# Expert weights in pieces of 4 contraction blocks by 512 columns instead of 8 by 256, and six units of work per expert instead of eight

## The chip, the cores and the metric

The kernel runs on one core of a Trainium2 chip. The metric is the device time of one execution in microseconds (us), the median of several runs. The engines are PE (TensorE, matrix products; its weight loads are shown apart as PEld), DVE (VectorE), ACT (ScalarE), POOL (GpSimd) and SP (SyncE, which here issues transfers). Each engine works through its own list of instructions in order and waits for the others by semaphores. Transfers run on 16 DMA engines.

## The reference

One layer of a diffusion trunk: a token mixer (windowed attention beside a long convolution), then a mixture of 32 experts of which each of 1024 tokens uses four. The change lies in the experts alone. Cut to them (D is 1024, D_FF is 1024, w1 is 1024 x 2048 and w2 is 1024 x 1024 per expert, all float32):

```python
logits = xt @ router_w + router_b
top_vals, top_idx = lax.top_k(logits, 4)
gate = softmax(top_vals)
...
for each expert e, on the tokens tok that chose it:
    hb = x[tok] @ w1[e] + b1[e]
    glu, lin = split(hb, 2)
    glu = minimum(glu, 7.0); lin = clip(lin, -7.0, 7.0)
    act = glu * sigmoid(1.702 * glu) * (lin + 1.0)
    acc[tok] += (act @ w2[e] + b2[e]) * weight
```

So column f of the gate half of w1 and column 1024 + f of its linear half meet in one value of `act`, and every value of `hb` is a sum over all 1024 rows of w1, which are 8 contraction blocks of 128 rows.

## The kernel before

**Stages.** Until about 1128 us the program computes the token mixer and the routing; the experts run from there to about 2503 us; the last 50 us add up and normalise. The change touches the experts.

**Experts by rank.** Experts are sorted by the number of their tokens; the expert of rank r gets `CAPS[r]` columns (line 68), from 416 down to 32. Two are in work at a time, in two lanes: lane 0 takes ranks 0, 1, 2, ... (416, 384, 304, 256, ... columns), lane 1 takes them from the end (32, 32, ... up to 128). `plan` (lines 75 to 91) lays down in which order units of the two lanes follow each other: it adds up a price for PE and one for DMA per unit and takes lane 0 when PE has less than DMA. An expert has 8 units: 4 of w1, each with a gate piece and a linear piece, then 4 of w2, each with one piece.

**Pieces.** A piece is 1 MB of float32 weights: all 8 contraction blocks by 256 columns, so that each transferred row is 1 KB (`w1`, `w2` in `wjobs`, lines 336 to 338). `jload` (line 301) has SP load it into one of 5 `raw` buffers. `jsplit` (line 307) turns it into two float16 parts, in two halves: ACT writes the high part `wh` (line 315), DVE then the low part `wl` (line 317); there are 5 buffers of each. `jget` hands out the next piece, `jahead(2)` (line 319) has the next two split behind a unit's matmuls.

**A unit of w1** (lines 366 to 402). For each 128 columns of the piece `mm3` (line 339) adds 24 matmuls in PSUM: 8 contraction blocks, each with high times high, high times low and low times high (the experts of 56 columns and fewer join two of them). Gate and linear products go to PSUM side by side. Then follows the activation: DVE adds the bias to both (`sg` line 387, `sl` line 388), ACT takes the sigmoid (`ss`, line 391), DVE multiplies (lines 392 and 393), ACT and DVE write the high and the low part of the result (`ah` line 397, `al` line 398). These are the moving operand of w2.

**A unit of w2** (lines 404 to 418) has 2 times 24 matmuls on one piece; ACT writes the result `yT`. At an expert's end `rows_out` transposes it and adds it to the tokens' rows with an indirect transfer from POOL (line 431).

**The next expert's tokens** are fetched beside the units of the one before it in the same lane, by steps (`prep_`, lines 288 to 295): step 1 builds one-hot rows `S`; at step 2 (and 3) PE multiplies them with the row table (line 262), DVE makes indices `gi` of it, and POOL starts the indirect transfer of the tokens' rows into `g` (line 277); at steps 5 to 7 (4 to 7 for more than 256 columns) PE transposes `g` (`tr`, line 286) and ACT writes it as `xT`, the moving operand of w1. Step u is emitted ahead of unit u (line 472). The biases `br` of an expert are loaded by SP (lines 355 and 356) and transposed by PE (line 358) at its start.

**Order.** The tile framework lays down each engine's order when the program is built, from the order of the calls, priorities and its own view of when operands are ready. The chip's engines then keep that order.

Of the kernel before, what the change touches and what calls it, by code (L numbers as in the profile page):

```python
# [19 lines left out]
ALU = mybir.AluOpType  # L20
# [73 lines left out]
assert sorted((r,u) for l,r,u in PLAN)==[(r,u) for r in range(NE) for u in range(8)]  # L94
class Moe:
# [205 lines left out]
    def jload(s):  # L301
        nc=s.nc
        src=s.jobs[s.jl_n]
        raw=s.ww.tile([128,8,256],F32,name="raw",bufs=s.NRAW)
        nc.sync.dma_start(raw,src())
        s.jraw[s.jl_n]=raw; s.jl_n+=1
    def jsplit(s):
        nc,wk=s.nc,s.wk
        raw=s.jraw.pop(s.js_n)
        wh=s.ww.tile([128,8,256],F16,name="wh",bufs=s.nwh); wl=s.ww.tile([128,8,256],F16,name="wl",bufs=s.nwh)  # L310
        for j in range(2):
            n=2*s.js_n+j; o=slice(j*4,j*4+4); pool=s.pools and n%s.lo_mod in s.lo_pool; sc=1.0 if pool else 64.0
# [17 lines left out]
    def wjobs(s,r,e=None):  # L330
# [19 lines left out]
    def expert_(s,C,p,reg,xT,chunks):  # L350
# [15 lines left out]
        for u in range(4):  # L366

            wg=s.jget(); wl=s.jget()
            nb=2 if C<=256 else 1
            for c0 in range(0,2,nb):  # L370
                if cat:
                    t=ps.tile([128,4,2,64],F32,name="acc",bufs=4); pg,pl=t[:,0:2,:,:C],t[:,2:4,:,:C]
                elif C<=128:
                    t=ps.tile([128,4,128],F32,name="acc",bufs=4); pg,pl=t[:,0:2,:C],t[:,2:4,:C]
                else:
                    pg=ps.tile([128,nb,512//nb],F32,name="acc",bufs=4)[:,:,:C]; pl=ps.tile([128,nb,512//nb],F32,name="acc",bufs=4)[:,:,:C]
# [3 lines left out]
                T2=lambda dt,name,bufs: wk.tile([128,max(2*PMAX[p],4*CCAT) if PMAX[p]<=256 else 512],dt,name=name+str(p),bufs=bufs)[:,:nb*C].rearrange("p (j c) -> p j c",j=nb)  # L380
                g=T2(F32,"sg",2); l=T2(F32,"sl",2); sg=T2(F32,"ss",1)
                for j in range(nb):
                    f=u*2+c0+j
                    if cat:
                        nc.vector.tensor_scalar(g[:,j],pg[:,j,0],bc[:,f:f+1],None,op0=ALU.add); nc.vector.tensor_scalar(l[:,j],pl[:,j,0],bc[:,8+f:9+f],None,op0=ALU.add)
                        continue
                    nc.vector.tensor_scalar(g[:,j],pg[:,j],bc[:,f:f+1],448.0,op0=ALU.add,op1=ALU.min)  # L387
                    nc.vector.tensor_scalar(l[:,j],pl[:,j],bc[:,8+f:9+f],512.0,op0=ALU.add,op1=ALU.min)  # L388
# [15 lines left out]
        for u in range(4):  # L404

            w=s.jget()
            for c in range(2):
                m=u*2+c
# [3 lines left out]
                if c==1: s.jahead(s.ahead)  # L412
# [8 lines left out]
    def nact(s,p,nb): return 9 if p==0 else 5  # L421
    def rows_out(s,C,chunks,yT):
# [10 lines left out]
    def experts(s,only=None):  # L433
# [8 lines left out]
        for i in range(-(-(CAPS[0]+128)//256)):  # L442
            raw=s.ww.tile([128,8,256],F32,name="raw",bufs=s.NRAW)
            G0+=[raw[:,4*h:4*h+4].rearrange("p a b -> p (a b)").bitcast(F16).rearrange("p (a d) -> p a d",a=2) for h in range(2)]
# [20 lines left out]
        for n,(l,r,u) in enumerate(P):  # L465
# [5 lines left out]
            if preps[l]:  # L471
                for f in preps[l][u]: f()
# [3 lines left out]
            if u==7: next(run[l],None)  # L476
# [473 lines left out]
class PhaseA2(PhaseA):  # L950
# [218 lines left out]
    def final(s,m,out):  # L1169
        nc,wk=s.nc,m.wk  # L1170
        g,b=s.l2; Y=[]
        for i in range(4):
            raw=m.ww.tile([128,8,256],F32,name="raw",bufs=m.NRAW).rearrange("p a b -> p (a b)")
# [209 lines left out]
```

## Time and profile before

| | |
|---|---|
| median of 3 runs | 2553.73 us (2553.55 to 2560.67) |
| the profiled execution, its own time | 2556.94 us |
| its span | 2555.1 us |
| granted TensorE clock, mean (1 is 2.4 GHz) | 0.922 |
| PE busy | 2206.9 us, 86% |
| DVE busy | 2118.1 us, 83% |
| ACT busy | 1462.0 us, 57% |
| POOL busy | 912.6 us, 36% |
| DMA, mean over the span | 594.26 MB at 233 GB/s |

The table is of the whole program. The shares of busy time are means over stages that differ; the experts' stage has to be read by itself, by the view that cuts the span into stretches and by who waited for whom in it. A matmul's duration in the trace is from issue to end and overlaps the next ones, so the pace of PE is read from counts over time.

### The profile page before, as it was taken

Reading aid. Unit: us, or ns where it says so; the run is one execution under the profiler, and the core shown is the slowest. Engines: PE = TensorE matmul, PEld = TensorE weight load, DVE = VectorE, ACT = ScalarE, POOL = GpSimd, SP = SyncE. Lnnn points to the kernel's source line nnn. Section 1 sums busy time; section 2 is a strip of 40 time slices with the busy share of each in tenths; the row PEclk is TensorE's granted clock in tenths of the full one; section 3 lists DMA queues with packets and bytes.
Section 4 is the critical chain, followed back from the end, with each engine's and each line's share of the span. In section 5 each row is a group of like instructions: output and inputs, shape, how many; then the busy total and the mean of one; then the engine's idle time right before and its main releaser. Section 6 shows DMA issues by size and latency. Waiting matters only on the chain. (4 is left out here: it accounts for less than half of the span.)

```text
span 2555.1 us, 60900 instructions
## 1 busy us (share of the span) xinstructions
PE 2206.9 (86%) x25050; PEld 1651.7 (65%) x25073; DVE 2118.1 (83%) x3669; ACT 1462.0 (57%) x2180; POOL 912.6 (36%) x593
## 2 busy tenths in 40 slices
PE   7888968698798989858898988998989999999991
PEld 4555454244354444435566666898989999999991
DVE  5867898978966835859989897989999998999984
ACT  3533234223145521446777767786877878888872
POOL 1544576765634844401121313313131121322214
PEclk9889989899879999868998989999999999999996
DMA  8424533444332333267999998999999999999984
GB/s 284 128 83 169 178 117 95 142 162 141 119 77 92 108 107 114 100 212 260 325 307 304 301 295 279 336 329 340 325 324 331 340 343 328 351 329 354 354 270 150
DMA packets 520403, 594.26 MB, mean 233 GB/s; under 512 B 16708, under 2 KB 472332, under 8 KB 520118
## 3 DMA queue, kind: packets, MB, share of 16 engines
q1 hardware_dynamic: 493432, 508.27, 59.6%
q0 software_dynamic: 13152, 43.69, 6.6%
q10 hardware_dynamic: 13534, 38.35, 4.4%
q8 instruction: 198, 3.24, 0.5%
q14 instruction: 87, 0.71, 0.1%
HBM read 532.95 MB, written 57.29 MB: 231 GB/s over the span
## 5 line engine op out<-in xcount | busy, mean ns | idle before, releaser
L317 DVE SCALAR_TENSOR_TENSOR wl<-raw,wh 128x1024 f16<-128x1024 f32 x768 | 910.0, 1214 | 64.0 <-ACT wh L315 56.6
L315 ACT ACTIVATE wh<-raw 128x1024 f16<-128x1024 f32 x768 | 768.9, 1049 | 209.5 <-PE acc L347 100.9
L347 PEld LDWEIGHTS <-wh 128*128 128x128 f16 x9984 | 788.1, 100 | 106.9 <-issue 31.8
L347 PE MATMUL acc<-xT,wh 128*128 128x80 f16 (+18 forms) x6656 | 721.0, 236 | 3.8 <-DVE yT L415 1.7
L347 PE MATMUL acc<-xT,wl 128*128 128x112 f16 (+19 forms) x3328 | 639.2, 235 | 1.1 <-DVE wl L317 1.1
L347 PEld LDWEIGHTS <-wl 128*128 128x128 f16 x4992 | 494.3, 100 | 48.6 <-issue 11.1
L431 POOL DMA_INDIRECT accD<-yr,si x49 | 126.3, 2578 | 726.5 <-ACT yr L430 526.3
L347 PE MATMUL acc<-ah,wh 128*128 128x112 f16 (+19 forms) x1664 | 332.3, 241 | 23.6 <-ACT ah L397 10.7
L811 PE MATMUL mm<-hx,wh 128*128 128x512 f16 (+1 forms) x1072 | 332.7, 389 | 18.9 <-ACT qx L865 9.6
L347 PE MATMUL acc<-al,wh 128*128 128x112 f16 (+19 forms) x1664 | 334.2, 241 | 7.2 <-DVE al L398 7.0
L347 PE MATMUL acc<-ah,wl 128*128 128x112 f16 (+19 forms) x1664 | 333.5, 241 | 0.0
L277 POOL DMA_INDIRECT g<-rows,gi x44 | 187.2, 4254 | 358.1 <-DVE tf L266 336.7
L811 PE MATMUL mm<-hx,wl 128*128 128x512 f16 x536 | 208.3, 389 | 17.3 <-POOL wl L796 17.3
L811 PEld LDWEIGHTS <-wh 128*128 128x128 f16 x1072 | 107.2, 100 | 138.4 <-issue 30.7
L724 DVE TENSOR_TENSOR bf<-bf 128x256 f32<-128x256 f32 (+1 forms) x232 | 167.5, 773 | 10.2 <-POOL bf L724 6.3
L416 ACT ACTIVATE yT<-acc,bc,g2s 128x112 f32<-128x112 f32 (+19 forms) x208 | 97.3, 483 | 25.8 <-PE acc L347 25.8
L811 PEld LDWEIGHTS <-wl 128*128 128x128 f16 x536 | 53.9, 100 | 87.5 <-POOL wl L796 20.6
L1010 POOL TENSOR_TENSOR pl<-pe,ph 128x512 f16<-128x512 f32 x60 | 74.7, 1261 | 84.1 <-ACT pe L1009 67.8
L795 POOL TENSOR_SCALAR wr<-wr 128x1024 f32<-128x1024 f32 x34 | 59.1, 1738 | 105.5 <-ACT wh L793 105.5
L344 PEld LDWEIGHTS <-wl 128*128 128x128 f16 x1152 | 80.1, 99 | 17.8 <-issue 15.9
L397 ACT ACTIVATE ah<-sl 128x64 f16<-128x64 f32 (+18 forms) x140 | 56.7, 408 | 60.7 <-DVE sl L393 60.1
L796 POOL TENSOR_TENSOR wl<-wr,wh 128x1024 f16<-128x1024 f32 (+1 forms) x49 | 87.5, 1799 | 2.5 <-PE mm L811 0.8
(400 smaller groups left out, 3990.6 us busy)
## 6 DMA issues: line engine op xcount, KB each, us to landing
raw<-in_exp_w SPq DMA_DIRECT2D x384, 1024.0 KB
wr<-in_w_in SPq DMA_DIRECT2D x34, 512.0 KB
t<-in_w_mod ACTq DMA_DIRECT2D x32, 512.0 KB
bf<-in_dec SPq DMA_DIRECT2D x32, 256.0 KB
Hd<-bf ACTq DMA_DIRECT2D x32, 256.0 KB
bf<-Hd SPq DMA_DIRECT2D x32, 256.0 KB
Gd<-t ACTq DMA_DIRECT2D x16, 512.0 KB
gt<-Gd SPq DMA_DIRECT2D x32, 256.0 KB
```

The source lines that it names most:

```text
L277: nc.gpsimd.indirect_dma_start(out=g[:cs].rearrange("p a d -> p (a d)"),out_offset=None,in_=s.rows,in_offset=bass.IndirectOffsetOnAxis(ap= ...
L315: else: nc.scalar.activation(wh[:,o],raw[:,o],AF.Copy,scale=sc)
L317: else: nc.vector.scalar_tensor_tensor(wl[:,o],raw[:,o],64.0,wh[:,o],op0=ALU.mult,op1=ALU.subtract)
L344: nc.tensor.matmul(ps_,wh,x[k],start=k==0,stop=False); nc.tensor.matmul(ps_[:,0],wl,x[k][:,0],start=False,stop=k==7)
L347: nc.tensor.matmul(ps_,a,b,start=n==0,stop=n==23); n+=1
L416: nc.scalar.activation(y,py,AF.Identity,bias=bc[:,16+m:17+m],scale=s.g2s[:,m:m+1])
L431: st=nc.gpsimd.indirect_dma_start(out=s.accD,out_offset=bass.IndirectOffsetOnAxis(ap=si[:cs,:1],axis=0),in_=yr[:cs],in_offset=None,compute ...
L724: (nc.gpsimd if pool and s.usepool else nc.vector).tensor_tensor(o,a,b,op=op)
L795: nc.gpsimd.tensor_scalar(raw,raw,64.0,0.0,op0=ALU.mult,op1=ALU.add)
L796: for H,L,R in parts: nc.gpsimd.tensor_tensor(L,R,H,op=ALU.subtract)
L811: nc.tensor.matmul(p,w[a][:,k,:],s.hx[b][:,k,o],start=i==0,stop=i==23); i+=1
L1010: (nc.gpsimd if n in s.plp else nc.vector).tensor_tensor(pl,pe,ph,op=ALU.subtract)
```

## The change

A piece is still 1 MB, but it is 4 contraction blocks by 512 columns: rows of 2 KB, and two pieces (blocks 0 to 3 and 4 to 7) hold what 128 columns of output need. An expert has six units of two pieces each: gate columns 0 to 511, linear columns 0 to 511, gate 512 to 1023, linear 512 to 1023, w2 columns 0 to 511, w2 512 to 1023. A gate unit ends with the gate's half of the activation (bias, sigmoid, product), whose result waits in `sg` (5 or 3 buffers instead of 2); the linear unit does the rest. The plan counts every unit as a sixth. The fetching steps 4 and 5 come ahead of unit 4, steps 6 and 7 ahead of unit 5. The number and shapes of the matmuls, splits and activation instructions stay. In the changed file the lines behind 336 are shifted: the split stays at 315 and 317, the matmuls are at 346 (343 for the smallest experts), the gate's operations at 387 to 391, the linear half's at 399 to 407.

```diff
@@ plan
-        r,u=cur[l]; f=1/6. if u<4 else 1/12.
+        r,u=cur[l]; f=1/6.
         pe+=pecost(CAPS[r])*k*f; dma+=dmacost(CAPS[r])*f
         out.append((l,r,u)); last=l
-        cur[l]=(r,u+1) if u<7 else None
+        cur[l]=(r,u+1) if u<5 else None
@@ jload, jsplit
-        raw=s.ww.tile([128,8,256],F32,name="raw",bufs=s.NRAW)
+        raw=s.ww.tile([128,4,512],F32,name="raw",bufs=s.NRAW)
...
-            n=2*s.js_n+j; o=slice(j*4,j*4+4); pool=...
+            n=2*s.js_n+j; o=slice(j*2,j*2+2); pool=...
@@ wjobs
-        w1=lambda o: (lambda: s.A['exp_w1'][ds(reg(),1)].rearrange("e (k p) f -> p (e k) f",p=128)[:,:,o:o+256])
-        w2=lambda o: (lambda: s.A['exp_w2'][ds(reg(),1)].rearrange("e (k p) f -> p (e k) f",p=128)[:,:,o:o+256])
-        return reg,[[w1(u*256),w1(1024+u*256)] for u in range(4)]+[[w2(u*256)] for u in range(4)]
+        w=lambda n,o: [(lambda k=k: s.A[n][ds(reg(),1)].rearrange("e (k p) f -> p (e k) f",p=128)[:,k:k+4,o:o+512]) for k in (0,4)]
+        return reg,[w('exp_w1',o) for o in (0,1024,512,1536)]+[w('exp_w2',o) for o in (0,512)]
@@ mm3
-            wh=w[0][:,k,c*128:(c+1)*128]; wl=w[1][:,k,c*128:(c+1)*128]
+            wh,wl=[t[:,k%4,c*128:(c+1)*128] for t in w[k//4]]
@@ expert_
-        for u in range(4):
-            wg=s.jget(); wl=s.jget()
...
-                for j in range(nb): s.mm3(pg[:,j],wg,c0+j,x,C)
-                for j in range(nb): s.mm3(pl[:,j],wl,c0+j,x,C)
-                if c0+nb==2: s.jahead(s.ahead)
+        def products(w):
+            for c0 in range(0,4,nb):
...
+                for j in range(nb): s.mm3(q[:,j],w,c0+j,x,C)
+                if c0+nb==4: s.jahead(s.ahead)
+                yield c0,q
+        for v in range(2):
+            G=[]
+            for c0,q in products((s.jget(),s.jget())):
+                g=T2(F32,"sg",s.nsg(p,nb)); sg=T2(F32,"ss",1)
...
+                nc.scalar.activation(sg,g,AF.Sigmoid,scale=1.702/64)
+                nc.vector.tensor_tensor(g,g,sg,op=ALU.mult)
+                G.append(g)
+            yield
+            for c0,q in products((s.jget(),s.jget())):
+                l=T2(F32,"sl",2); g=G.pop(0)
...
@@ expert_, w2
-        for u in range(4):
-            w=s.jget()
-            for c in range(2):
+        for v in range(2):
+            w=(s.jget(),s.jget())
+            for c in range(4):
@@ experts
-                for f in preps[l][u]: f()
+                for f in preps[l][u] if u<4 else preps[l][2*u-4]+preps[l][2*u-3]: f()
...
-            if u==7: next(run[l],None)
+            if u==5: next(run[l],None)
```

**PE, where a unit goes from its first piece to its second.** Lane 0, the rank with 192 columns, its first unit of w1 (`xT0` are the tokens, `acc` the sum in PSUM, the number behind `wh` or `wl` tells the pieces apart). Before, the last matmul on the gate piece and the first on the linear piece:

```order
L347 LDWEIGHTS wl_28436
L347 MATMUL acc_28540<-xT0_27866,wl_28436 128x192
L347 LDWEIGHTS wh_28509
L347 MATMUL acc_28541<-xT0_27866,wh_28509 128x192
L347 LDWEIGHTS wh_28509
```

Now, the first place in the unit where the second piece is needed:

```order
L346 LDWEIGHTS wl_28502
L346 MATMUL acc_28540<-xT0_27658,wl_28502 128x192
L346 LDWEIGHTS wh_28507
L346 MATMUL acc_28540<-xT0_27658,wh_28507 128x192
L346 LDWEIGHTS wh_28507
```

Before, 48 of the unit's 96 matmuls stood ahead of this point, and the sum changed with the piece. Now 12 stand ahead of it, within one sum, and the unit comes back to the first piece for the next 128 columns; its last use of the first piece is matmul 84.

**PE, where the next tokens of lane 1 are transposed.** Lane 1 has rank 17 in work and fetches for rank 16, both of 112 columns; lane 0 has rank 7, of 192 columns. `g1` holds the fetched rows, `ah1` and `al1` are operands of w2 of rank 17, `xT0` of w1 of rank 7. Before:

```order
L347 MATMUL acc_29524<-al1_28942,wh_29467 128x112
L347 LDWEIGHTS wl_29468
L347 MATMUL acc_29524<-ah1_28941,wl_29468 128x112
L286 LDWEIGHTS g1_29094
L286 MATMUL tp_29569<-idh_67,g1_29094 128x112
```

Now:

```order
L346 LDWEIGHTS wl_29327
L346 MATMUL acc_29424<-xT0_27658,wl_29327 128x192
L286 LDWEIGHTS g1_29094
L286 MATMUL tp_29496<-idh_67,g1_29094 128x112
```

Before, the transposes stood within the expert's second unit of w2; now they stand ahead of its first. Between the matmuls that make the row indices (line 262) and these transposes PE had 312 matmuls of w1 and w2 (216 with 112 columns, 96 with 192); it now has 168 (144 and 24).

**DVE, the end of w1 of rank 17.** Before, the end of the chain to `al1_29347`, the last operand that w2 needs (`gi` and `S0` are of a gather for lane 0):

```order
L393 SCALAR_TENSOR_TENSOR sl1_29210<-sl1_29210,sg1_29209 128x224
L392 TENSOR_TENSOR sg1_29336<-sg1_29336,ss1_29338 128x224
L264 CAST gi_29722<-tp_29713 40x1
L392 TENSOR_TENSOR sg0_29483<-sg0_29483,ss0_29485 128x384
L266 TENSOR_SCALAR tf_29724<-tp_29713,dum_81 40x1
L254 TENSOR_TENSOR S0_31211<-io16_77,posm_11091 128x8x24
L393 SCALAR_TENSOR_TENSOR sl1_29337<-sl1_29337,sg1_29336 128x224
L398 SCALAR_TENSOR_TENSOR al1_29220<-sl1_29210,ah1_29219 128x224
L393 SCALAR_TENSOR_TENSOR sl0_29484<-sl0_29484,sg0_29483 128x384
L267 TENSOR_TENSOR si_29726<-tf_29724,tp_29713 40x1
L269 TENSOR_REDUCE gc_29728<-tp_29713 40x1
L398 SCALAR_TENSOR_TENSOR al1_29347<-sl1_29337,ah1_29346 128x224
```

Now, from the last bias of the linear half (`sl1_29342`) to the same operand:

```order
L399 TENSOR_SCALAR sl1_29342<-acc_29221,bc_28671 128x112 x2
L407 SCALAR_TENSOR_TENSOR al1_29275<-sl1_29270,ah1_29274 128x224
L391 TENSOR_TENSOR sg1_29215<-sg1_29215,ss1_29216 128x224
L317 SCALAR_TENSOR_TENSOR wl_29480<-raw_29213,wh_29479 128x1024 x2
L402 SCALAR_TENSOR_TENSOR sl1_29342<-sl1_29342,sg1_29215 128x224
L317 SCALAR_TENSOR_TENSOR wl_29623<-raw_29338,wh_29622 128x1024
L387 TENSOR_SCALAR sg0_29418<-acc_29369,bc_28536 128x192 x2
L317 SCALAR_TENSOR_TENSOR wl_29623<-raw_29338,wh_29622 128x1024
L387 TENSOR_SCALAR sg0_29489<-acc_29424,bc_28536 128x192 x2
L317 SCALAR_TENSOR_TENSOR wl_29629<-raw_29340,wh_29628 128x1024 x2
L407 SCALAR_TENSOR_TENSOR al1_29347<-sl1_29342,ah1_29346 128x224
```

Before, six splits (`wl`) and a build of `S0` stood between the last bias of the linear half and the first row shown; no split stands in the rows shown. Now six splits stand in the chain as well, and neither build of `S0`; the gate's last product still stands in it.

## Rows read from the trace of the kernel before

**Rows 1.** The page, part 1: busy us (share of the span) xinstructions.
```profile
PE 2206.9 (86%) x25050; PEld 1651.7 (65%) x25073; DVE 2118.1 (83%) x3669; ACT 1462.0 (57%) x2180; POOL 912.6 (36%) x593
```

**Rows 2.** Busy us by stretch; the last three columns are granted clock, DMA share, GB/s.
```profile
core 0: us, PE busy (x) PEld busy (x) DVE busy (x) ACT busy (x) POOL busy (x), PEclk, DMA share, GB/s
...
1128.00:1600.00 472.00, 423.33 (x5229) 303.11 (x5228) 416.87 (x875) 329.45 (x471) 98.02 (x28) 0.92 0.89 291
1600.00:2400.00 800.00, 759.50 (x12040) 739.92 (x12036) 745.26 (x1208) 635.07 (x858) 195.84 (x56) 0.97 1.02 337
2400.00:2503.00 103.00, 98.99 (x1546) 97.15 (x1544) 84.20 (x135) 76.80 (x108) 17.84 (x8) 0.98 0.81 265
```

**Rows 3.** What PE waited for, 1128 to 2500: us in total, times, longest.
```profile
PE tp L286 <- DMA g<-rows,gi: 16.4, 4, 5.4
PE tp L358 <- DMA br<-in_exp_b: 10.8, 7, 3.1
PE acc L347 <- ACT ah L397: 10.7, 6, 3.6
PE acc L344 <- DVE ah L398: 9.9, 6, 3.1
PE acc L347 <- DVE al L398: 7.0, 4, 3.3
...
PE acc L347 <- DVE sl L388: 5.8, 4, 2.7
...
PE acc L347 <- ACT wh L315: 1.3, 1, 1.3
...
PE acc L347 <- DVE wl L317: 1.1, 1, 1.1
```

**Rows 4.** What ACT waited for, 1128 to 2500.
```profile
ACT wh L315 <- PE acc L347: 100.9, 94, 8.6
...
ACT wh L315 <- DMA raw<-in_exp_w: 27.6, 21, 4.7
```

**Rows 5.** The page, part 5: the two halves of the split.
```profile
L317 DVE SCALAR_TENSOR_TENSOR wl<-raw,wh 128x1024 f16<-128x1024 f32 x768 | 910.0, 1214 | 64.0 <-ACT wh L315 56.6
L315 ACT ACTIVATE wh<-raw 128x1024 f16<-128x1024 f32 x768 | 768.9, 1049 | 209.5 <-PE acc L347 100.9
```

**Rows 6.** Queue of the weights, 2000 to 2100: packets, MB, share of 16 engines.
```profile
q1 hardware_dynamic: 31556, 31.71, 92.2%
```

**Rows 7.** The same queue, 850 to 900.
```profile
q1 hardware_dynamic: 2090, 4.18, 26.6%
```

**Rows 8.** The queue that ACT issues on, 900 to 1000.
```profile
q10 hardware_dynamic: 576, 2.10, 5.7%
```

**Rows 9.** Index matmuls of one gather (line 262), 2081 to 2083.
```profile
L262 PE MATMUL tp<-M,S x8: 168/191/191, 2081.9 to 2082.2; 128*112 128x4 f16 x8
```

**Rows 10.** Timeline of POOL, 2080 to 2112: start, us.
```profile
2085.27 4.88 POOL L277 DMA_INDIRECT g<-rows,gi  x1 [7.44 <-DVE tf L266]
```

**Rows 11.** All gathers of the experts (tile g): from issue to landing.
```profile
DMA to landing us min/median/max: 4.9/9.9/26.9
```

**Rows 12.** Transposes of that gather's rows (line 286), 2100 to 2103.
```profile
L286 PE MATMUL tp<-idh,g x11: 209/212/214, 2101.0 to 2103.0; 112*128 112x112 f16 x11
```

**Rows 13.** Busy us between the two, columns as in rows 2.
```profile
2082.20:2101.00 18.80, 18.80 (x325) 18.80 (x324) 18.80 (x34) 13.80 (x17) 6.89 (x2) 1.00 1.06 347
```

**Rows 14.** The chain that ended last: start, us; one unit with 120 columns.
```profile
2262.06 5.15 PE acc L347 x96
```

More of the change, by code (lines that the diff above doesn't have):

```diff
@@ L87, in plan @@
         if cur[l] is None: l=1-l
-        r,u=cur[l]; f=1/6. if u<4 else 1/12.
+        r,u=cur[l]; f=1/6.
         pe+=pecost(CAPS[r])*k*f; dma+=dmacost(CAPS[r])*f
         out.append((l,r,u)); last=l
-        cur[l]=(r,u+1) if u<7 else None
+        cur[l]=(r,u+1) if u<5 else None
 PLAN=plan()
 PMAX=[max(CAPS[r] for l,r,u in PLAN if l==k) for k in range(2)]
-assert sorted((r,u) for l,r,u in PLAN)==[(r,u) for r in range(NE) for u in range(8)]
+assert sorted((r,u) for l,r,u in PLAN)==[(r,u) for r in range(NE) for u in range(6)]
 class Moe:
@@ L309, in jsplit @@
         raw=s.jraw.pop(s.js_n)
-        wh=s.ww.tile([128,8,256],F16,name="wh",bufs=s.nwh); wl=s.ww.tile([128,8,256],F16,name="wl",bufs=s.nwh)
+        wh=s.ww.tile([128,4,512],F16,name="wh",bufs=s.nwh); wl=s.ww.tile([128,4,512],F16,name="wl",bufs=s.nwh)
         for j in range(2):
-            n=2*s.js_n+j; o=slice(j*4,j*4+4); pool=s.pools and n%s.lo_mod in s.lo_pool; sc=1.0 if pool else 64.0
+            n=2*s.js_n+j; o=slice(j*2,j*2+2); pool=s.pools and n%s.lo_mod in s.lo_pool; sc=1.0 if pool else 64.0
             if pool: nc.gpsimd.tensor_scalar(raw[:,o],raw[:,o],64.0,0.0,op0=ALU.mult,op1=ALU.add)
@@ L365, in expert_ @@
         ah,al=[],[]
-        for u in range(4):
-            wg=s.jget(); wl=s.jget()
-            nb=2 if C<=256 else 1
-            for c0 in range(0,2,nb):
+        nb=2 if C<=256 else 1
+        T2=lambda dt,name,bufs: wk.tile([128,max(2*PMAX[p],4*CCAT) if PMAX[p]<=256 else 512],dt,name=name+str(p),bufs=bufs)[:,:nb*C].rearrange("p (j c) -> p j c",j=nb)
+        def products(w):
+            for c0 in range(0,4,nb):
                 if cat:
-                    t=ps.tile([128,4,2,64],F32,name="acc",bufs=4); pg,pl=t[:,0:2,:,:C],t[:,2:4,:,:C]
+                    if c0==0: t=ps.tile([128,4,2,64],F32,name="acc",bufs=4)
+                    q=t[:,c0:c0+2,:,:C]
@@ L381, in expert_ @@
-                g=T2(F32,"sg",2); l=T2(F32,"sl",2); sg=T2(F32,"ss",1)
-                for j in range(nb):
[L383 to L388, printed above, removed]
+                    if c0==0: t=ps.tile([128,4,128],F32,name="acc",bufs=4)
@@ new lines, in expert_ @@
+                G.append(g)
+            yield
+            for c0,q in products((s.jget(),s.jget())):
+                l=T2(F32,"sl",2); g=G.pop(0)
+                for j in range(nb):
+                    f=v*4+c0+j
+                    if cat: nc.vector.tensor_scalar(l[:,j],q[:,j,0],bc[:,8+f:9+f],None,op0=ALU.add)
+                    else: nc.vector.tensor_scalar(l[:,j],q[:,j],bc[:,8+f:9+f],512.0,op0=ALU.add,op1=ALU.min)
+                if cat:
+                    nc.vector.tensor_tensor(l,l,q[:,:,1],op=ALU.add); nc.vector.tensor_scalar(l,l,512.0,None,op0=ALU.min)
@@ L411, in expert_ @@
                 s.mm3(py,w,c,ah if cat else (ah,al),C)
-                if c==1: s.jahead(s.ahead)
+                if c==3: s.jahead(s.ahead)
                 y=T(F32,"yT",8)
@@ L421, in nact, with nsg @@
     def nact(s,p,nb): return 9 if p==0 else 5
+    def nsg(s,p,nb): return 5 if p==0 else 3
     def rows_out(s,C,chunks,yT):
@@ L442, in experts @@
         for i in range(-(-(CAPS[0]+128)//256)):
-            raw=s.ww.tile([128,8,256],F32,name="raw",bufs=s.NRAW)
-            G0+=[raw[:,4*h:4*h+4].rearrange("p a b -> p (a b)").bitcast(F16).rearrange("p (a d) -> p a d",a=2) for h in range(2)]
+            raw=s.ww.tile([128,4,512],F32,name="raw",bufs=s.NRAW)
+            G0+=[raw[:,2*h:2*h+2].rearrange("p a b -> p (a b)").bitcast(F16).rearrange("p (a d) -> p a d",a=2) for h in range(2)]
         nraw=s.nraw; s.nraw=nraw-len(G0)//2; s.pools=False
@@ L1172, in final @@
         for i in range(4):
-            raw=m.ww.tile([128,8,256],F32,name="raw",bufs=m.NRAW).rearrange("p a b -> p (a b)")
+            raw=m.ww.tile([128,4,512],F32,name="raw",bufs=m.NRAW).rearrange("p a b -> p (a b)")
             Y+=[raw[:,:1024],raw[:,1024:]]
```

14 lines of the change are left out of this document (7 added, 7 removed).

## The prediction

> **What bounds the kernel now.** I read the page's part 1 first [rows 1]. PE with 86% and DVE with 83% are means over three stages, so I cut the span at the experts' begin and end [rows 2]. There the shares are: PE busy 423.3 of 472 us, 759.5 of 800 and 99.0 of 103; DVE 416.9, 745.3 and 84.2; DMA share 0.89, 1.02 and 0.81. The reader is to see three resources that are all nearly full, in one stage of 1375 us, in which PE is idle for 1375 - 1281.8 = 93 us. Busy shares don't tell which of the three paces the others, so the next view is what PE waited for in this stage [rows 3]. PE waited 1.3 and 1.1 us in all for the split weights (`wh` and `wl`), but 16.4 us for gathered rows, 10.8 us for biases, and 10.7 + 9.9 + 7.0 + 5.8 = 33.4 us for the activation between w1 and w2. So the weights reach PE in time nearly always. The opposite wait is large: ACT stood 100.9 us because PE had not yet released a `wh` buffer, and only 27.6 us because a piece had not landed [rows 4]. The bound is therefore PE with the operands that arrive by gather and activation, with DVE close behind; the transfers have some slack, and the weights' stock of split pieces (5 buffers) is what keeps it so.
>
> **The change part by part**, against the profiled execution's own 2556.9 us; the median of the runs is 3.2 us lower, which I take off at the end.
>
> *Splits, matmuls, activation.* 768 splits on DVE at 1.214 us and 768 on ACT at 1.049 us stay [rows 5], since half a piece is 1024 columns either way; the matmuls and the activation keep count and shape. Nothing is added or removed: 0, without cover.
>
> *Transfers.* In the fullest stretch the weights' queue moved 31.71 MB in 92.2% of 16 engines and 100 us, that is 46.5 us of one engine per MB [rows 6]. All 384 pieces (402.7 MB) take 402.7 x 46.5 / 16 = 1170 us of the 16 engines. No row shows 2 KB packets alone at full load. Packets of 2.0 KB on a mostly idle queue took 0.266 x 16 x 50 / 4.18 = 50.9 us per MB [rows 7], 9% more; packets of 3.6 KB on another took 0.057 x 16 x 100 / 2.10 = 43.4 us, 7% less [rows 8]. So transfer time changes by -80 to +105 us, and I take 4% less, nearer to the larger packets, because the 2 KB row is of an unloaded queue. Little of it is on the path: ACT has a fifth of its time free [rows 2], and PE met only the two waits for biases and gathers, 27.2 us together [rows 3]. On the path the ends are -27 (both waits gone) and +28 (ACT's 27.6 us again, all of it passed on to PE). I take -4, a seventh of the first, as a queue that is 4% shorter still has the same order.
>
> Beside this stands the Trainium skill, DMA: Bandwidth & Descriptors, section "Why small descriptors are slow (HBM only)": the engine's inner bus has a fixed overhead of about 3 cycles per packet beside one per 32 bytes. Worked out from it, 1 KB takes 35 cycles and 2 KB 67, 4.3% less per byte, an estimate that lies between the two rows; were the transfers the end of the path, it would be 49 us off the sum, and the forecast would change sign. The waits in rows 3 and 4 speak against that here; rival A has the case.
>
> *The fetch of the next tokens.* Steps 4 and 5 now come ahead of unit 4, so PE reaches the transposes earlier. For rank 16, the index matmuls ended at 2082.2 [rows 9], POOL issued the gather at 2085.3 [rows 10], and PE came to the transposes at 2101.0 [rows 12]. A gather lands 9.9 us after its issue in the median [rows 11], so the rows were there some 3.1 + 9.9 = 13.0 us after the index matmuls, and PE came after 18.8 us, all of it busy, with 325 matmuls at 57.8 ns each [rows 13]. The changed order leaves 168 matmuls there, 9.7 us at that price: PE comes 3.3 us early and waits. Counted in this way for all gathers, with each matmul priced by its width (5.15 us for 96 of 120 columns, 0.45 ns per column [rows 14]), 11 of the 44 gathers in the changed order have less than 13.0 us, with 37 us missing in all; before, 3 had, with 5 us missing (16.4 us were waited for, as single gathers took up to 26.9 us). The ends: 0, if PE is held up by other things in these places, so that the rows are in time; +42 if the missing 32 us are paid in full and late gathers cost 10 us more. I take +18, a little over half of 32, because one of the 11 lies between the smallest experts, where the splits pace PE anyway.
>
> *Two pieces per sum.* A unit now needs its second piece after 12 matmuls instead of 48, and gives its first piece back after 84 instead of 48. Below, the end is 0: the wait for `wh` and `wl` was 2.4 us before, so the stock was ahead by more than that. Above, every unit of lane 0's three widest experts (416, 384 and 304 columns) waits for its second piece as long as the 36 matmuls take that no longer lie ahead: 36 x 6 x 0.45 ns x 1104 columns = 107 us. I take +12, near to the row, since it shows PE hardly ever waiting.
>
> *Activation.* The gate's sigmoid and product are now started a unit earlier, but in the changed order six splits stand between the last bias and the last `al1`, as many as before, and only the two builds of one-hot rows are gone. The ends are -33 (all four waits of rows 3) and 0; I take 0, because the same six splits, 7.3 us, still fill that chain.
>
> Sum: -4 + 18 + 12 + 0 = +26, so 2582.9 for a profiled execution and **2580 us** for the median.
>
> **The rivals.** *A, the transfers pace it after all, faster.* For it: the DMA share of 1.02 in the longest stretch, and PE's idle 93 us, which would follow the transfers. Against it: 2.4 us of PE's waits are for weights. If half of the idle time goes and the fetch costs nothing: 2556.9 - 46 = about 2510. *B, the activation gains, faster.* Half of its 33.4 us goes (-17), the transfers give -4, and the fetch and the stock cost nothing: 2533. Against it stand the six splits in the chain. *C, gains and costs cancel*: within 8 us of 2553.7. This is also what a change that does not do what it says would leave, if the hardware cut the 2 KB rows in two again and the fetch were in time. *D, the stock runs dry, much slower.* In units of the widest experts PE waits at matmul 13 for the second piece, ACT then stands longer for buffers, and two thirds of the 107 us are paid: 2556.9 + 18 + 70 - 4 - 3 = 2638. It decides where, at the start of such a unit, fewer than one and a half pieces are split ahead. For it speaks that 100.9 us of ACT's time already go into waiting for buffers; against it, rows 3.
>
> By the Trainium skill's TensorE: Matmul & The Clock Gate, section "HAM oscillation — how this bites in real kernels", one should finish all contraction tiles of an output tile before waiting for the next load; the change parts each output tile's contraction over two loads, so this rule points to D, its 2638. The granted clock of 0.97 and the 2.4 us bear out that PE does not wait for loads before the change; what it does after, no row shows.
>
> **How the numbers follow.** My forecast (2562 to 2605) has 0.43, D 0.15, C 0.15, B 0.15 and A 0.12. So faster has 0.27, the same 0.15 and slower 0.58, where 0.3% (8 us) is about what a measurement of this kernel can tell from no change. The range of 2525 to 2640 leaves out most of A and half of D, about 0.18, and holds the bounds of the single terms as far as they don't meet in one direction.
>
> **What would show it.** In the changed profile, PE's wait for `g` should be near 16 + 18 = 34 us and its wait for `wh` and `wl` near 14 us. Packets under 2 KB should fall by about 390,000, and the weights' queue should need 44 to 45 us per MB. The activation's four waits should stay near 33 us. I am wrong if the wait for `g` does not grow (its step falls), if PE's wait for weights is above 60 us (D), or if ACT's wait for pieces goes away and PE's idle time falls by more than 30 us with it (A).

## The result, and the profile after

The changed kernel takes 2616.9 us (median of 4 runs, 2611.9 to 2622.2) against 2553.6 for the kernel before: a ratio of 1.0242 with a 95% interval of 1.0218 to 1.0266. Slower was forecast, and 2616.9 lies in the stated range, but the forecast of 2580 held 26 us of loss where 63 came. The profiled execution took 2614.6 us, 57.7 more than that of before.

The page, part 1, of the changed kernel, beside [rows 1]:

```profile
PE 2209.9 (85%) x25072; PEld 1645.6 (63%) x25073; DVE 2118.7 (81%) x3669; ACT 1458.2 (56%) x2180; POOL 849.7 (33%) x593
```

The work of PE, DVE and ACT is the same, as forecast: PE is busy 3 us longer, DVE 0.6 us, ACT 3.8 us less. (POOL has the same 593 instructions and 63 us less busy time; its durations are rough, and nothing here rests on them.) What came is 58 us of idle time. Busy us by stretch, beside [rows 2]; the experts now end at 2557:

```profile
1128.00:1600.00 472.00, 401.87 (x4866) 283.88 (x4864) 402.75 (x857) 311.90 (x440) 69.19 (x28) 0.92 0.79 270
1600.00:2400.00 800.00, 727.95 (x11487) 701.60 (x11486) 703.94 (x1135) 601.76 (x822) 150.24 (x52) 0.97 0.94 321
2400.00:2557.00 157.00, 150.72 (x2424) 148.05 (x2422) 138.66 (x223) 119.62 (x168) 27.24 (x11) 1.00 0.87 299
```

PE was busy for 1280.5 of 1429 us, so it stood 148.5 us where it stood 93: 55 of the 57.7 us are here. The granted clock is 0.92, 0.97 and 1.00 where it was 0.92, 0.97 and 0.98, so the loss is not one of TensorE's clock. Note also the DMA share: 0.79 for 0.89 and 0.94 for 1.02 in the two long stretches, in which no engine is busier than before either.

What PE waited for from 1128 to 2557 (us in total, times, longest), beside [rows 3]:

```profile
PE tp L286 <- DMA g<-rows,gi: 44.0, 10, 17.7
PE tp L357 <- DMA br<-in_exp_b: 16.4, 11, 2.9
PE acc L346 <- ACT yT L424: 16.3, 12, 2.6
PE acc L346 <- DVE al L407: 14.6, 11, 3.6
PE acc L343 <- DVE yT L423: 11.4, 9, 3.0
PE acc L346 <- DVE wl L317: 11.2, 16, 2.5
PE acc L346 <- ACT ah L406: 5.2, 2, 3.5
PE acc L343 <- DVE wl L317: 3.4, 5, 1.1
...
PE acc L343 <- ACT yT L424: 1.4, 2, 0.9
PE acc L346 <- DVE yT L423: 1.4, 1, 1.4
...
PE acc L346 <- DVE sl L399: 0.4, 2, 0.3
```

And the same view before, for the sums of w2 that leave PSUM through `yT`, which stood in no group:

```profile
PE acc L347 <- ACT yT L416: 5.5, 8, 2.1
PE acc L347 <- DVE yT L415: 3.1, 3, 1.7
PE acc L344 <- DVE yT L415: 2.5, 2, 2.3
PE acc L344 <- ACT yT L416: 2.2, 2, 1.9
```

Read alone, these rows seem to confirm the forecast and to add one item: `g` rose by 27.6 us (forecast 18, "near 34"), the split weights from 2.4 to 14.6 ("near 14"), `yT` from 13.3 to 30.5, the biases by 5.6; the activation (`ah`, `al`) fell from 27.6 to 19.8. The experiments show that this reading is wrong: a row names who came last, and taking away what it names need not give the time back.

The opposite view is what DVE waited for. Before, 1128 to 2500:

```profile
DVE wl L317 <- ACT wh L315: 43.7, 67, 2.8
...
DVE sg L387 <- PE acc L347: 13.0, 11, 4.5
...
DVE sl L388 <- PE acc L347: 8.8, 9, 2.8
```

After, 1128 to 2557:

```profile
DVE wl L317 <- ACT wh L315: 62.1, 53, 4.6
DVE sg L387 <- PE acc L346: 37.9, 25, 6.9
DVE sl L399 <- PE acc L346: 37.7, 16, 15.5
...
DVE sg L386 <- PE acc L343: 7.2, 6, 3.7
DVE sl L398 <- PE acc L343: 3.9, 3, 3.0
```

DVE now stands 86.7 us at biases of w1 whose sum PE has not finished (the last four rows; 21.8 before), with splits queued behind them in its order. And ACT's wait for buffers, beside [rows 4]:

```profile
ACT wh L315 <- PE acc L346: 145.5, 80, 20.6
...
ACT wh L315 <- DMA raw<-in_exp_w: 3.7, 2, 3.3
```

It waits longer for PE (145.5 for 100.9) and hardly any more for pieces (3.7 for 27.6). So PE waits for DVE, ACT and transfers, and DVE and ACT wait for PE, by turns.

### The profile page after: what moved, and what is told of

Its sections match the earlier page's. It is cut to its first block, busy times and chain, and to the rows that moved or that the text cites. A ratio compares the mean times of both kernels' runs of the same rounds, so it can differ in the third digit from the quotient of the medians.

```text
span 2612.9 us, 60913 instructions
## 1 busy us (share of the span) xinstructions
PE 2209.9 (85%) x25072; PEld 1645.6 (63%) x25073; DVE 2118.7 (81%) x3669; ACT 1458.2 (56%) x2180; POOL 849.7 (33%) x593
## 2 busy tenths in 40 slices
DMA packets 323795, 594.26 MB, mean 227 GB/s; under 512 B 16708, under 2 KB 79116, under 8 KB 323510
## 5 line engine op out<-in xcount | busy, mean ns | idle before, releaser
L315 ACT ACTIVATE wh<-raw 128x1024 f16<-128x1024 f32 x768 | 756.9, 1048 | 185.3 <-PE acc L346 145.5
L346 PE MATMUL acc<-xT,wh 128*128 128x120 f16 (+19 forms) x6656 | 734.3, 237 | 7.7 <-DVE cs L232 2.5
L346 PEld LDWEIGHTS <-wl 128*128 128x128 f16 x4992 | 491.6, 99 | 68.5 <-issue 17.6
L440 POOL DMA_INDIRECT accD<-yr,si x49 | 105.5, 2153 | 742.8 <-ACT yr L439 465.8
L346 PE MATMUL acc<-al,wh 128*128 128x112 f16 (+19 forms) x1664 | 323.5, 237 | 14.6 <-DVE al L407 14.6
L346 PE MATMUL acc<-ah,wl 128*128 128x112 f16 (+19 forms) x1664 | 319.1, 237 | 0.9 <-DVE wl L317 0.7
L277 POOL DMA_INDIRECT g<-rows,gi x44 | 144.1, 3274 | 470.0 <-DVE tf L266 380.9
L820 PEld LDWEIGHTS <-wl 128*128 128x128 f16 x536 | 53.7, 100 | 89.9 <-POOL wl L805 22.5
L406 ACT ACTIVATE ah<-sl 128x64 f16<-128x64 f32 (+19 forms) x140 | 56.7, 409 | 93.0 <-DVE sl L402 92.9
L387 DVE TENSOR_SCALAR sg<-acc,bc 128x112 f32<-128x112 f32 (+19 forms) x208 | 71.2, 377 | 38.1 <-PE acc L346 37.9
L390 ACT ACTIVATE ss<-sg 128x64 f32<-128x64 f32 (+18 forms) x140 | 57.2, 409 | 80.2 <-DVE sg L387 53.2
L399 DVE TENSOR_SCALAR sl<-acc,bc 128x112 f32<-128x112 f32 (+19 forms) x208 | 70.8, 376 | 37.7 <-PE acc L346 37.7
```

The lines of the kernel that those rows point to most:

```text
L277: nc.gpsimd.indirect_dma_start(out=g[:cs].rearrange("p a d -> p (a d)"),out_offset=None,in_=s.rows,in_offset=bass.IndirectOffsetOnAxis(ap= ...
L315: else: nc.scalar.activation(wh[:,o],raw[:,o],AF.Copy,scale=sc)
L346: nc.tensor.matmul(ps_,a,b,start=n==0,stop=n==23); n+=1
L387: else: nc.vector.tensor_scalar(g[:,j],q[:,j],bc[:,f:f+1],448.0,op0=ALU.add,op1=ALU.min)
L399: else: nc.vector.tensor_scalar(l[:,j],q[:,j],bc[:,8+f:9+f],512.0,op0=ALU.add,op1=ALU.min)
L440: st=nc.gpsimd.indirect_dma_start(out=s.accD,out_offset=bass.IndirectOffsetOnAxis(ap=si[:cs,:1],axis=0),in_=yr[:cs],in_offset=None,compute ...
```

## The experiments

Ratios are to the kernel before, run beside each of these kernels on the same chip, with 95% intervals. Cuts in the code are marked by three dots.

### Which part of the change costs

**The fetch (e1).** One more break in each w2 unit gives the fetch its eight places back:

```diff
+                if c==1: yield
...
-                for f in preps[l][u] if u<4 else preps[l][2*u-4]+preps[l][2*u-3]: f()
-            next(run[l])
+                for f in preps[l][u] if u<4 else preps[l][2*u-4]: f()
+            next(run[l])
+            if u>3:
+                if preps[l]:
+                    for f in preps[l][2*u-3]: f()
+                next(run[l])
```

> The changed kernel, with the fetch of the next tokens spread over eight places again (one more break in the middle of each unit of w2). Theory 1 (fetch: the changed kernel's 44.0 us of PE waiting for gathered rows against 16.4 before are the missing distance between index matmuls and transposes, and gathers queued behind scatters on POOL): the wait for g falls to 16 to 22 us and the time by 20 to 28 us, to about 2592. Theory 2 (units of two pieces in w2: PE's waits for yT, 31.7 us against 13.3, and for split weights, 14.9 against 2.7): the g wait may fall, but PE then waits for those operands instead and the time falls by less than 8 us, above 2609.

Measured: 2618.4 us, ratio 1.0228 (1.0210 to 1.0247): no gain that can be told from none, as theory 2 had it. But the wait for `g` stayed too:

```profile
PE tp L286 <- DMA g<-rows,gi: 39.9, 7, 17.7
PE tp L357 <- DMA br<-in_exp_b: 18.6, 13, 3.1
```

The longest wait, 17.7 us, is at the same place as the longest in the changed kernel. POOL's timeline in the changed kernel, 1470 to 1515 (start, us; idle time before, and what ended it):

```profile
1475.03 1.94 POOL L440 DMA_INDIRECT accD<-yr,si  x1 [9.46 <-ACT wh L315]
1485.60 3.12 POOL L440 DMA_INDIRECT accD<-yr,si  x1 [8.63 <-issue]
1497.21 4.21 POOL L440 DMA_INDIRECT accD<-yr,si  x1 [8.49 <-ACT wh L315]
1501.72 0.97 POOL L277 DMA_INDIRECT g<-rows,gi  x1 [0.30 <-issue]
```

The index matmuls of this gather ended near 1483. The gather is issued 18.9 us later, since it stands behind three scatters on POOL, 10.6 and 11.6 us apart. For this wait, the largest single part of the 44.0 us, it was the queue, not the distance in matmuls, that made the gather late; for the other 26 us this was not followed up.

**The rows of 2 KB (e4).** Each piece is loaded as two halves of 256 columns:

```diff
-        nc.sync.dma_start(raw,src())
+        d=src()
+        for h in range(2): nc.sync.dma_start(raw[:,2*h:2*h+2].rearrange("p a b -> p (a b)").rearrange("p (k f) -> p k f",k=4),d[:,:,256*h:256*h+256])
...
```

> The changed kernel with each piece loaded by two transfers of 256 columns, so rows of 1 KB again; order, splits and matmuls unchanged. If the transfers lie beside the path in the changed kernel (ACT waited only 3.7 us for pieces): within 10 us of the changed kernel, 2607 to 2627, while the weights' queue goes back to 46 us per MB at full load. If the 2 KB rows give a gain on the path that hides a larger loss elsewhere: 2635 or more, with ACT's wait for pieces above 25 us and more than 5 us of waits for it passed on to PE.

Measured: 2617.7 us, ratio 1.0248 (1.0214 to 1.0282): no difference from the changed kernel that could be told, with intervals of 0.24% and 0.34% to either side. The weights' queue from 2300 to 2400 (packets, MB, share of 16 engines) in the changed kernel:

```profile
q1 hardware_dynamic: 15406, 30.34, 83.8%
```

with 1 KB rows (e4):

```profile
q1 hardware_dynamic: 31774, 31.45, 91.9%
```

and in the kernel before:

```profile
q1 hardware_dynamic: 31816, 31.98, 92.5%
```

That is 0.838 x 1600 / 30.34 = 44.2 us of one engine per MB against 46.8 and 46.3. The transfers did become cheaper, and the time shows none of it.

**w1 alone and w2 alone (e2, e3).** e2 keeps the changed w1 and returns to four w2 units of one piece; e3 the other way round, with six units.

```diff
 e2, against the changed kernel
...
-        return reg,[w('exp_w1',o) for o in (0,1024,512,1536)]+[w('exp_w2',o) for o in (0,512)]
+        return reg,[w('exp_w1',o) for o in (0,1024,512,1536)]+[[(lambda o=o: s.A['exp_w2'][ds(reg(),1)].rearrange("e (k p) f -> p (e k) f",p=128)[:,:,o:o+256])] for o in range(0,1024,256)]
...
 e3, against the kernel before
...
-        return reg,[[w1(u*256),w1(1024+u*256)] for u in range(4)]+[[w2(u*256)] for u in range(4)]
+        return reg,[[w1(u*256),w1(1024+u*256)] for u in range(4)]+[[w2(k,o) for k in (0,4)] for o in (0,512)]
...
```

> w1 as in the changed kernel (pieces of 4 blocks by 512 columns, gate half and linear half apart), w2 as before (four units of one piece of 8 by 256), so eight units and eight fetch places. Theories 1 and 2 (the loss is in the fetch and in w2's units): the waits for g and yT are back near 16 and 13 us, and the time is 2555 to 2575. Theory 3 (the loss is in w1: two pieces per sum, and gate and linear apart): it stays above 2595, with 12 us or more of waits for split weights.

> w1 as before (gate and linear piece of 8 by 256 in each unit), w2 as in the changed kernel (two units of two pieces of 4 by 512), six units and the fetch in six places. Theories 1 and 2: 2600 to 2620, with g near 44 us and yT near 30 us. Theory 3: below 2575.

Measured: 2621.0 us, ratio 1.0243 (1.0226 to 1.0260), for w1 alone, and 2581.5, ratio 1.0103 (1.0074 to 1.0132), for w2 alone. Theory 3: w1 alone brings the whole loss, with the old eight fetch places and the old w2. The two losses, 64 and 24 us, are together more than that of the whole change.

**The two halves of the change in w1 (e5, e7).** e5 takes gate and linear apart but keeps pieces of 8 by 256; e7 keeps gate and linear in one unit, but a piece is 4 blocks of 256 gate and 256 linear columns, so that each sum takes two pieces.

```diff
 e5, against the changed kernel (with eight units and one-piece w2)
...
-            wh,wl=[t[:,k%4,c*128:(c+1)*128] for t in w[k//4]]
+            wh,wl=[t[:,k,c%2*128:c%2*128+128] for t in w[c//2]]
...
 e7, against the kernel before
...
-        return reg,[[w1(u*256),w1(1024+u*256)] for u in range(4)]+[[w2(u*256)] for u in range(4)]
+        return reg,[[w1(u*256,0),w1(u*256,4)] for u in range(4)]+[[w2(u*256)] for u in range(4)]
...
```

> The kernel before with one part of the change alone: w1's units go by gate half (two gate pieces) and then linear half (two linear pieces), with the changed kernel's activation code, but all pieces stay 8 by 256 columns, so that each sum needs one piece and a piece is free after 48 matmuls; w2, eight units and fetch as before. Theory S (stock: the loss in w1 comes from two pieces per sum, which holds the first piece until matmul 84 and so shortens the stock of split pieces): near the kernel before, 2550 to 2575. Theory O (order: the loss comes from gate and linear apart, which changes what the in-order queues of DVE and ACT do between the splits): 2600 to 2625, like the run with w1 alone changed (2621).

> The kernel before with the other part alone: a w1 piece is 4 contraction blocks of 256 gate and 256 linear columns (two transfers of 512 KB, rows of 1 KB), so each sum needs two pieces and both are held to the unit's end, while units, activation and w2 stay as before. Theory S: 2595 to 2625, with ACT's wait for buffers (100.9 us before) above 130 us. Theory O: 2550 to 2575.

Measured: apart alone 2560.3 us, ratio 1.0016 (0.9998 to 1.0035); two pieces per sum alone 2588.1, ratio 1.0124 (1.0090 to 1.0158). e5 and e2 differ in the pieces of w1 alone: 2560 and 2621. Theory O falls. The pieces are what costs, though e7 lost less than theory S said, and ACT's wait for buffers did not rise there:

```profile
ACT wh L319 <- PE acc L351: 91.6, 62, 8.9
```

The two halves don't add up either. Apart alone costs 0.2% and two pieces alone 1.2%, but both together, in e2, 2.4%: two pieces per sum cost about twice as much where gate and linear are apart.

**One piece per sum in the changed kernel (e6).** Loads, six units, gate and linear apart and fetch stay; a split reads half the columns of two landed pieces:

```diff
-        raw=s.jraw.pop(s.js_n)
-        wh=s.ww.tile([128,4,512],F16,name="wh",bufs=s.nwh); wl=s.ww.tile([128,4,512],F16,name="wl",bufs=s.nwh)
+        i,h=s.js_n//2*2,s.js_n%2; R=[s.jraw[i+j][:,:,h*256:h*256+256] for j in range(2)]
+        wh=s.ww.tile([128,8,256],F16,name="wh",bufs=s.nwh); wl=s.ww.tile([128,8,256],F16,name="wl",bufs=s.nwh)
...
-            wh,wl=[t[:,k%4,c*128:(c+1)*128] for t in w[k//4]]
+            wh,wl=[t[:,k,c%2*128:c%2*128+128] for t in w[c//2]]
```

> The changed kernel with its loads (4 by 512, rows of 2 KB), six units, gate and linear apart and fetch, but the split pieces are 8 by 256 again: a split reads half the columns of two landed pieces, so that each sum needs one split piece, which is free after 48 of the unit's 96 matmuls. Number and size of splits as in the changed kernel. Theory P (two pieces per sum are the loss, in w1 and in w2): 2550 to 2570, and DVE's waits for sums of PE fall from 88 us to 50 or less. Theory G (the rest of the loss is the six-unit grain): 2575 to 2595. If two pieces per sum are not the cause: above 2605.

Measured: 2558.4 us, ratio 1.0010 (0.9993 to 1.0027). The whole loss is gone, with the six fetch places, the plan of six units and the 2 KB rows still there. What PE waited for:

```profile
PE tp L354 <- DMA br<-in_exp_b: 17.4, 13, 4.2
...
PE tp L286 <- DMA g<-rows,gi: 6.9, 2, 4.5
```

and what DVE waited for:

```profile
DVE sg L384 <- PE acc L343: 20.4, 17, 4.8
...
DVE sl L396 <- PE acc L343: 5.2, 8, 2.1
...
DVE sg L383 <- PE acc L340: 2.2, 2, 1.7
...
DVE sl L395 <- PE acc L340: 1.1, 3, 0.5
```

DVE's waits at biases are back to 28.9 us on these four lines (86.7 in the changed kernel), and the wait for `g` is 6.9, in six fetch places. So theory P: two split pieces per sum are the cause.

### How two pieces per sum cost

**Where in the unit (x1).** The w1-only kernel e2, with the first piece used for two sums before the second:

```diff
...
-                for j in range(nb): s.mm3(q[:,j],w,c0+j,x,C)
...
+                    for h in range(2):
+                        for j in range(2): s.mmh(q[j],w[h],h,c0+j,x)
...
```

> The run with w1 alone changed (2621), with the matmuls of w1 in another order for all experts of more than 56 tokens: the first piece's blocks for two sums, then the second piece's for the same two, so the second piece is needed after 24 matmuls for 12 and the first is free after 72 for 84. Sums of a unit lie in twice the PSUM banks where they were one bank. Theory P in the form that the places of first need and last use count (distance from a buffer's release to the need of the piece that fills it, 120 matmuls in the run with w1 alone, 144 here, 192 before): 2575 to 2600. If only that a sum needs two pieces counts, not where: 2610 to 2630.

Measured: 2616.1 us, ratio 1.0225 (1.0199 to 1.0250), 5 us under e2, with intervals that overlap. The places of first need and last use, as far as these 12 matmuls go, are not it; but this kernel also spreads the sums of a unit over twice the PSUM banks, and what that does was not measured by itself.

**How many buffers (e8, x4, e9).**

```diff
 e8, the changed kernel
-    NRAW=nraw=5; nwh,rawkeep=5,1
+    NRAW=nraw=4; nwh,rawkeep=6,1
 x4, the changed kernel
-    NRAW=nraw=5; nwh,rawkeep=5,1
+    NRAW=nraw=4; nwh,rawkeep=5,1
 e9, the kernel before
-    NRAW=nraw=5; nwh,rawkeep=5,1
+    NRAW=nraw=5; nwh,rawkeep=4,1
```

> The changed kernel with six buffers of split pieces for five, and four raw buffers for five (the memory of the core does not hold both). Theory S: the longer stock gives back most of the loss, 2565 to 2590, and ACT's wait for buffers falls below 110 us. Theory O: less than 10 us, above 2605.

> The changed kernel with four raw buffers for five and the five split buffers left, the partner of the run with six split and four raw buffers (2609). Theory P in the form of distances (a sixth buffer takes 120 matmuls to 204): 2630 to 2660, so that the sixth buffer is worth 20 to 50 us at equal raw buffers. If the number of buffers does not count: 2605 to 2620.

> The kernel before with four buffers of split pieces for five, nothing else. Theory S (the kernel hangs on this stock): 2590 to 2640, with waits for g and yT that grow although fetch and order are untouched. Theory O: below 2575.

Measured: 2609.4 us, ratio 1.0206 (1.0171 to 1.0241); 2611.1, ratio 1.0199 (1.0171 to 1.0227); 2566.5, ratio 1.0043 (1.0024 to 1.0061). Theory S and the distances of theory P miss in all three. A sixth split buffer is worth nothing beside four raw buffers, and four split buffers for five cost the kernel before 10 us, a third of the least that was expected. In e8 ACT waited much longer for pieces than in the changed kernel (3.7 us),

```profile
ACT wh L315 <- DMA raw<-in_exp_w: 60.4, 51, 5.3
```

so a gain may have been lost there; a sixth buffer beside five raw ones was not tried.

**The order of PE (x7, x8, x9).** Each sum of the experts is held behind the one traced before it, by an order edge without a wait:

```diff
...
+        if s.lastmm is None or not s.inorder: return s.mm3_(ps_,w,c,x,C)
+        with s.tc.issue_after(s.lastmm): s.mm3_(ps_,w,c,x,C)
...
```

> The changed kernel, with the matmuls of the experts held to the order of the program (an order edge from each sum to the one traced before it, no wait): PE does unit after unit as the plan has them. In the changed kernel's order PE switches between the lanes 309 times (before 209, with split pieces of 8 by 256 233), often within a sum, so that two units are open at once and on average 2.46 of the 5 split buffers are held by open units (1.07 before, 1.07 with 8 by 256, 1.46 with two pieces per sum alone, 2.31 with w1 alone). Held to the plan it is 1.73. Theory M (the loss comes by the open units, which hold the stock): 2575 to 2605. If two pieces per sum cost by themselves, in whatever order: 2608 to 2630. If the mixing was a help: above 2630.

> The kernel before with the same order edges (held pieces 1.00 for 1.07). Theory M: within 10 us of before, 2547 to 2567. If order edges themselves cost, for PE can't fill a gap with the other lane: 2570 or more; this run is the control of the one above.

> The changed kernel with split pieces of 8 by 256 (2558) and the same order edges: held pieces 0.88. Theory M: 2540 to 2560, at least as fast as before. If the edges cost: 2570 or more.

Measured: the changed kernel 2723.6 us, ratio 1.0659 (1.0636 to 1.0681); the kernel before 2600.4, ratio 1.0188 (1.0166 to 1.0210); one piece per sum 2678.3, ratio 1.0481 (1.0458 to 1.0503). Theory M falls as far as it makes the mixing the harm: mixing the lanes is a help, worth 46 us before and over 100 here. In the same held order, two pieces per sum still cost 2723.6 - 2678.3 = 45 us. What does go with the loss is the number of split buffers that open units hold, by the counts above: 1.07 before and in e6 (loss 0 and 2 us), 1.46 in e7 (32), 2.31 in e2 (64), 2.46 in the changed kernel (63), and 1.73 against 0.88 in the two held orders that differ by 45 us. No run changes this number alone.

**The lead of the splits (y1, y2, y3).** DVE does splits and biases in one fixed order. Go through it, and at each bias of a w1 sum count the pieces whose splits stand ahead of it; take off the pieces that PE, in its own order, has begun by that sum's last matmul. The mean over all biases is the lead: 3.63 pieces before, 2.59 in e6, 1.21 in the changed kernel, where an open unit has begun two pieces at once and frees both near its end. These runs take the lead away by fewer split buffers, with one piece per sum:

```diff
 y1 and y2, the kernel e6; y3, the kernel before
-    NRAW=nraw=5; nwh,rawkeep=5,1
+    NRAW=nraw=5; nwh,rawkeep=4,1
+    NRAW=nraw=5; nwh,rawkeep=3,1
```

(four buffers in y1, three in y2 and y3).

> The same with four split buffers, lead 1.76, between the two. Theory L: 2570 to 2605. If two pieces per sum cost by themselves: 2553 to 2568.

> The changed kernel with split pieces of 8 by 256 (2558, one piece per sum), with three split buffers for five. Counted in the order of instructions, at each bias that DVE takes from a sum of w1 so many pieces have been split beyond those that PE has begun by that sum: 3.63 on average before, 2.59 with pieces of 8 by 256, 1.21 in the changed kernel, 1.03 here. Theory L (what counts is this lead of the splits in DVE's order, in whatever way it is lost: with a short lead each stall of PE or DVE is passed on to the other): 2605 to 2640, with DVE's waits for sums at 70 us or more. If a sum that takes two pieces costs by itself: below 2590.

> The kernel before with three split buffers for five (with four it took 2567), lead 1.73. Theory L: 2575 to 2615. If two pieces per sum cost by themselves: below 2575.

Measured:

| kernel | lead | us | ratio (95%) |
|---|---|---|---|
| e6, five buffers | 2.59 | 2558.4 | 1.0010 (0.9993 to 1.0027) |
| y1, e6 with four | 1.76 | 2589.3 | 1.0142 (1.0117 to 1.0166) |
| y2, e6 with three | 1.03 | 2656.6 | 1.0402 (1.0378 to 1.0425) |
| y3, before with three | 1.73 | 2594.5 | 1.0156 (1.0129 to 1.0182) |
| the changed kernel | 1.21 | 2616.9 | 1.0242 (1.0218 to 1.0266) |

Theory L has the times of y1 and y3, and y2 lies above its range. The changed kernel, with 1.21, falls between 1.76 and 1.03. But the waits are others. What PE waited for in y2:

```profile
PE tp L354 <- DMA br<-in_exp_b: 40.3, 25, 4.8
PE tp L286 <- DMA g<-rows,gi: 25.5, 7, 6.0
PE acc L340 <- DVE wl L314: 22.0, 27, 2.0
PE acc L343 <- DVE wl L314: 19.9, 26, 2.0
PE acc L343 <- ACT wh L313: 18.1, 20, 1.9
```

60.0 us go to split weights here, 14.6 in the changed kernel, and what DVE waited for in y2 is below the 70 us that were expected:

```profile
DVE sg L384 <- PE acc L343: 33.1, 21, 6.6
DVE sl L396 <- PE acc L343: 13.8, 17, 2.4
...
DVE sg L383 <- PE acc L340: 6.1, 3, 3.1
...
DVE sl L395 <- PE acc L340: 3.5, 4, 2.2
```

On all four lines of biases these are 56.5 us, against 86.7 in the changed kernel. So taking away split buffers can cost as much as was lost, and the changed kernel has a short lead. That the lead is the way in which two pieces per sum cost is not shown: e3 and e7 lose 24 and 32 us with leads of 3.51 and 2.97, and from x4 to e8 the lead rises from 1.16 to 1.73 with no gain. The lead is also a rough measure. It is counted from the order of the programs, not from a trace, and moves with where a sum is taken to end: with the last matmul of each 128 columns of output it is 3.9 before, 3.3 in e6, 2.3 in y1, 1.7 in y3 and 1.4 in both y2 and the changed kernel, whose times differ by 40 us.

### The biases loaded earlier (z1)

e6, with each expert's biases loaded just ahead of its first piece:

```diff
...
+                s.regs[r],W[r]=s.wjobs(r); g=W[r][0][0]
+                def first(r=r,g=g): s.brs[r]=s.brload(s.regs[r]()); return g()
+                W[r][0][0]=first
...
```

> The changed kernel with split pieces of 8 by 256 (2558), and with each expert's biases loaded just ahead of its first weight piece for at its first unit: PE's 17.4 us of waits for br there should be below 3 us. If this wait is on the path that sets the end: 2540 to 2550, faster than both kernels. If the splits' chain on DVE takes its place: 2553 to 2562.

Measured: 2551.7 us, ratio 0.9975 (0.9956 to 0.9994). The interval ends below 1, but 0.25% is less than the 0.3% that a measurement of this kernel can tell, so that it is faster than the kernel before is likely and not shown; and 2551.7 lies between the two ranges that were expected. PE's wait for biases fell from 17.4 to 3.0 us:

```profile
PE tp L359 <- DMA br<-in_exp_b: 3.0, 2, 1.8
```

Against e6 the ratio is lower by 0.35%, 9 us, with intervals that just meet, for 14.4 us of this wait taken away. So some of this wait was probably on the path; how much of it stays open.

## Why the prediction was right and wrong

*Splits, matmuls, activation: 0.* Right: busy times agree within 3 us on PE and 1 us on DVE.

*Transfers: -4.* Not contradicted: 1 KB rows in the changed kernel take 2617.7 for 2616.9 us, and with their intervals the runs can't tell -1 from -4. Packets under 2 KB fell from 472,332 to 79,116, by 393,216, and 44.2 us per MB lie in the forecast 44 to 45. The estimate from the Trainium skill, DMA: Bandwidth & Descriptors, section "Why small descriptors are slow (HBM only)", was 4.3% less per byte (which is 50 us of the 1170, not 49); the queue gives 1 - 44.2 / 46.3 = 4.5% against the kernel before and 5.6% against e4, so the trace agrees. Rival A falls: half of its sign came, for ACT's wait for pieces went from 27.6 to 3.7 us, but PE's idle time rose by 55 us, and cheaper transfers gave no time.

*The fetch: +18.* Wrong, though its sign in the trace was met. The step that failed is the one from a short distance in matmuls to a wait that costs time. The wait for `g` rose to 44.0, but the eight places of e1 gave nothing back (2618.4 us), and e6 has the six places and waits 6.9 us: the term measured nothing. Counting 11 gathers with under 13.0 us of matmuls left out that a gather can stand behind scatters on POOL, which is what made the longest wait.

*Two pieces per sum: +12, ends 0 and +107.* The right part of the change, with the wrong size and too narrow a way of costing: 2616.9 - 2558.4 = 58 us, this term alone nearly the whole loss. What failed is the reason for the value, "near to the row, since it shows PE hardly ever waiting". The wait for split weights did come out at 14.6, as forecast, and yet it was no measure of the price: it rose by 12.2 us, a fifth of the 58. The rest is booked on other rows, DVE's at unfinished sums and PE's at biases, gathers and `yT`; in e6 DVE's waits and those for gathers are back, those for biases are not (17.4 us). By what chain two pieces make these waits the runs don't show. A row of 2.4 us said that the stock was sufficient, not how much of it could be taken away. Runs with fewer split buffers would have shown that it has a price: 10 us for one buffer (e9), 40 for two (y3).

*Activation: 0.* Right in size by itself: taking gate and linear apart costs 4 us (interval from 0 to 9) in e5. But with two pieces per sum it is not nothing: e2 and e7 differ by it (and by the width of the loads), 2.4% against 1.2%, some 30 us; the sum added the two terms singly. The four waits that were to stay near 33 us came to 20.2 (`al` 14.6, `ah` 5.2, `sl` 0.4), and no time came of it.

*The sum.* +26 was made of a term that was not there (18) and one that was a fifth of its size (12 for 58). That the forecast came as near as it did, with 18 of its 26 us from that first term, was luck. *Rival D*, 2638, was the nearest in kind: it named the stock. Its own sign, over 60 us of waits for weights, did not come; y2, where the stock is cut by buffers, has 60.0 on the three rows shown. The rule of the Trainium skill, TensorE: Matmul & The Clock Gate, section "HAM oscillation — how this bites in real kernels", pointed to D. Its advice, given for products with few rows, is to do all contraction tiles of an output tile before waiting for the next load. The runs agree for split pieces and not for loads: in e6 each contraction still spans two loads, and one split piece per sum gives the 58 us back. The clock, which the page gives as the reason, is not it here: the granted clock did not fall in any of the three stretches (0.92, 0.97, 1.00).

## What to carry to other kernels

When two in-order engines are both nearly full, as PE and DVE are here, a wait row of 2 us on the buffers between them says that there are enough of them, not that some are free: price them by taking buffers away, before a change does so in another form. In this kernel split tiles had to be cut so that a sum finishes within one of them, while the load ahead could be wider than the split. And waits that grow in the places a forecast named are no proof of its cause until that place is undone alone.

## What was not expected

Holding PE to the order of the plan costs 46 us in the kernel before and 120 us with gate and linear apart (2678.3 against 2558.4): switching between the lanes within units, which looked like the disorder behind the loss, is a help. Nor was it expected that w1 alone (2621.0) and the whole change (2616.9) cost the same, while w2 alone cost 24 us.
